# Score products of a query tile issued in turn, and low weight halves of an FFN kept in DRAM, in a two-layer decoder trunk

## The chip, the cores and the metric

The kernel runs on one core of a Trainium2 chip. Its engines are TensorE (PE in the profile, its weight loads PEld), VectorE (DVE), ScalarE (ACT), GpSimd (POOL) and SyncE (SP), which here only issues transfers (DMAs). The metric is the device time of one execution in microseconds; the program is one launch.

## The reference, cut to what matters

Two layers run over 1024 tokens of width 1024. Each layer is a normalised and modulated mixer with a gated residual, then a SwiGLU feed-forward network (FFN) of hidden width 2816, again with a gated residual. The first layer's mixer is half a state-space model, half differential attention with 4 heads; the second layer's is an RWKV-7 recurrence.

```python
# differential attention, one block of 128 queries; c is one of two components of 64 columns
s = jnp.einsum('bqhcd,bkhcd->bhcqk', q_blk, kf[:, :kv_len]) * scale
p = jax.nn.softmax(jnp.where(mask, s, -jnp.inf), axis=-1)
w = p[:, :, 0] - lam * p[:, :, 1]
...
def swiglu(h, w_gate, w_up, w_down):
    return (jax.nn.silu(h @ w_gate) * (h @ w_up)) @ w_down
...
for l in range(DEPTH):
    ...
    x = x + gate_m * mix
    h = rms_norm(x, norm_ffn[l]) * (1.0 + scale_f) + shift_f
    x = x + gate_f * swiglu(h, ffn_w_gate[l], ffn_w_up[l], ffn_w_down[l])
```

## The kernel before

The 1024 tokens are two blocks of 512. Dense products take their operands as two rounded halves: `wsplit` (L442) loads a tile of weights with SP (`wraw`, L446), ScalarE casts it to the high half (`whi`, L449), and VectorE, or GpSimd where the caller says so, subtracts to get the low half (`wlo`, L450). Each of the three tags has two buffers, so a tile's buffer is free again when the tile two before it is done with. `mm3g` (L460) then issues three products per 128 rows of weights: high by high, high weight by low activation, low weight by high activation (L466). A gate or up tile is 1024 rows by 128 columns (512 KB, 24 products), a down tile 384 or 512 rows by 128 columns (9 or 12 products).

The FFN (`ffn`, L495) walks 22 columns of tiles in six chunks; a chunk is the gate and up tiles of 3 or 4 columns, then eight down tiles. Both blocks of tokens use the same weights, each in a pass of its own, so each weight tile is loaded and split twice.

The order of the work is written as generators that are woven: `weave(main, fill, rate)` takes `rate` steps of `fill` for each step of `main`, and a step of an FFN is three products. From the end of the first mixer on, TensorE's instructions stand in the order of the code (`manual_schedule`); the other engines' order, and TensorE's before that point, is set by a scheduler that models the run. The stages that matter here, with their times in the profiled execution:

- 210 to 400 us: attention of the first four query tiles (512 tokens) of each head, between the projections that feed it. TensorE's order is the scheduler's.
- 400 to 520 us: the gated unit of block 0, the output projection, and the first steps of the attention of block 1. TensorE's order is still the scheduler's.
- 520 to 1010 us: block 0's pass of the first layer's FFN (its weight halves split by VectorE), woven with the attention of block 1's query tiles (until 780 us) and then with the second layer's modulation vectors (`mods_acc`, 48 tiles of 512 KB that GpSimd's queue loads, 750 to 920 us).
- 1226 to 1907 us: block 0's recurrence (`rwkv_algebra`, 16 units of short dependent steps over TensorE, VectorE, ScalarE and GpSimd) with block 1's pass of the first layer's FFN as filling, whose low halves GpSimd makes.
- 2124 to 2780 us: the same for block 1's recurrence, filled with block 0's pass of the second layer's FFN, less its last eight down tiles.

In the attention, `attn_scores` (L988) takes one query tile of one head: for each of the two components it takes a bank pair `sps`, issues the products of the queries and keys (64 rows of the array: component 0 on rows 0 to 63, component 1 on rows 64 to 127; L1001) in pieces of at most 512 keys, adds the causal mask of the last 128 keys with a product by the identity (L1006), and then VectorE takes the maximum (L1010) and ScalarE the exponential (L1015). After each component it yields, so that other work stands between the two components. Values (L1039, L1044) follow one step later, the output transpose (L1062) two steps later.

SP issues in its own order and waits in it: a load that waits for its buffer holds back all that stand behind it on SP, which are the weight tiles and, in the recurrence, the loads `ks`, `rr`, `RV`, `wa`, `g2w` of its units and the store `zd`.

Of the kernel before, what the change touches and what calls it, by code (L numbers as in the profile page):

```python
# [8 lines left out]
F32 = mybir.dt.float32  # L9
# [9 lines left out]
P = 128  # L19
D = 1024  # L20
S = 1024
KT = D // P
TB = 512
# [66 lines left out]
def chain(*gens):  # L90
    for g in gens:
        yield from g


def lockstep(*gens):

    gens = list(gens)
    while gens:
        for g in gens[:]:
            if next(g, gens) is gens:  # L100
                gens.remove(g)
        yield
# [19 lines left out]
class Tall:  # L122


    def __init__(self, tiles):
        self.t = tiles
# [20 lines left out]
class Trunk:  # L147
    def __init__(self, ctx, tc, A, out, stages):
        self.ctx, self.tc, self.nc, self.A, self.out = ctx, tc, tc.nc, A, out
        self.stages = stages  # L150
        self.nid = 0
        self.guards = []

    def nm(self, s):
        self.nid += 1
        return f"{s}_{self.nid}"
# [282 lines left out]
            yield  # L439


    def wsplit(self, src, shape, eng=None):  # L442

        nc = self.nc
        raw = self.wp.tile(shape, F32, tag="wraw", name=self.nm("wraw"))
        nc.sync.dma_start(raw, src)  # L446
        hi = self.wp.tile(shape, F32R, tag="whi", name=self.nm("whi"))
        lo = self.wp.tile(shape, F32R, tag="wlo", name=self.nm("wlo"))
        nc.scalar.copy(hi, raw)  # L449
        (eng or nc.vector).tensor_tensor(lo, raw, hi.bitcast(F32), op=ALU.subtract)  # L450
        return hi, lo

    def mm3(self, out, whi, wlo, xhi, xlo, nk, first=True, last=True):

        drain(self.mm3g(out, whi, wlo, xhi, xlo, nk, first, last))
# [37 lines left out]
    def ffn(self, l, st, chunks, eng=None, parts="ud", dtag="B"):  # L493

        nc, A = self.nc, self.A  # L495
        wg, wu, wd = A["ffn_w_gate"][l], A["ffn_w_up"][l], A["ffn_w_down"][l]
        gate = self.mod[l][:, 40:48]
        tp, x = self.tp, st["x"]
        hh, hl = st["h"]
        if "d" not in st:  # L500
            st["d"] = [self.page([P, 4, TB], F32R, "dd", dtag) for _ in range(2)]
        dd = st["d"]
        for f0, f1 in chunks:
            nf = f1 - f0
            for f in range(f0, f1) if "u" in parts else ():
                yield from next(self.inject, ())
                pp, gens = [], []
                for w, nme in ((wg, "pg"), (wu, "pu")):
                    hi, lo = self.wsplit(w[:, f * P : (f + 1) * P].rearrange("(k p) n -> p k n", p=P), [P, KT, P], eng)
                    pt = self.ps.tile([P, TB], F32, tag="mm", name=self.nm(nme))  # L510
                    g = self.mm3w(pt, hi, lo, hh, hl, KT)
                    if f:
                        yield from g
                    gens.append(g)
                    pp.append(pt)
                if not f:
                    yield from lockstep(*gens)

                sg = tp.tile([P, TB], F32, tag="t0", name=self.nm("sg"))
                nc.scalar.activation(sg, pp[0], AF.Tanh, scale=0.5)  # L520
                nc.vector.scalar_tensor_tensor(sg, sg, 1.0, pp[0], op0=ALU.add, op1=ALU.mult)  # L521
                hd = tp.tile([P, TB], F32, tag="t1", name=self.nm("hd"))
                nc.vector.scalar_tensor_tensor(hd, pp[1], 0.5, sg, op0=ALU.mult, op1=ALU.mult)
                nc.scalar.copy(dd[0][:, f - f0, :], hd)
                nc.vector.tensor_tensor(dd[1][:, f - f0, :], hd, dd[0][:, f - f0, :].bitcast(F32), op=ALU.subtract)
            if "d" in parts:

                def down(n):
                    hi, lo = self.wsplit(
                        wd[f0 * P : f1 * P, n * P : (n + 1) * P].rearrange("(k p) n -> p k n", p=P), [P, nf, P], eng  # L530
                    )
                    pd = self.ps.tile([P, TB], F32, tag="mm", name=self.nm("pd"))
                    yield from self.mm3w(pd, hi, lo, dd[0], dd[1], nf)
                    nc.vector.scalar_tensor_tensor(x[:, n, :], pd, gate[:, n : n + 1], x[:, n, :], op0=ALU.mult, op1=ALU.add)  # L534
                    if l == 0 and f1 == NF:
                        self.square(x[:, n, :], n)

                d0, d1 = down(0), down(1)
                yield from self.some(d0, nf - 1)
                yield from self.some(d1, nf - 1)  # L540
                yield from chain(d0, d1, *(down(n) for n in range(2, KT)))
# [446 lines left out]
    def attn_scores(self, b, hd, i, st, ap, pss):  # L988
        nc = self.nc
        v = nc.vector  # L990
        qT, kT = self.qT[b], self.kT[hd // 2]
        kv = (i + 1) * P
        o = i * P - b * TB
        st["pe"], st["l"] = [], []
        for c in range(2):
            r = 64 * c
            sp = pss.tile([P, S if b else TB], F32, tag="s", name=self.nm("sps"))
            for c0 in range(0, kv, 512):
                n = min(512, kv - c0)
                last = c0 + n >= kv  # L1000
                nc.tensor.matmul(  # L1001
                    sp[:, c0 : c0 + n], lhsT=qT[r : r + 64, hd, o : o + P], rhs=kT[r : r + 64, hd % 2, c0 : c0 + n],
                    start=True, stop=not last, skip_group_check=True,
                )
                if last:
                    nc.tensor.matmul(  # L1006
                        sp[:, i * P : kv], lhsT=self.ident_b, rhs=self.cmask, start=False, stop=True, skip_group_check=True
                    )
            mx = ap.tile([P, 1], F32, tag="mx", name=self.nm("mx"), bufs=4)
            v.tensor_reduce(mx, sp[:, 0:kv], axis=AX.X, op=ALU.max)  # L1010
            nm = ap.tile([P, 1], F32, tag="nmx", name=self.nm("nmx"), bufs=4)
            v.tensor_scalar(nm, mx, -0.125, None, op0=ALU.mult)
            pe = self.pe[c][:, self.ne % 2, :]
            l = ap.tile([P, 1], F32, tag="l", name=self.nm("l"), bufs=6)
            nc.scalar.activation(pe[:, 0:kv], sp[:, 0:kv], AF.Exp, bias=nm, scale=0.125, accum_out=l)  # L1015
            st["pe"].append(pe)
            st["l"].append(l)
            yield
        self.ne += 1
# [843 lines left out]
```

## Time and profile before

| what | value |
|---|---|
| median of 3 runs | 3262.19 us (3261.68 to 3269.7) |
| profiled execution | 3254.43 us, span 3252.6 us |
| TensorE busy | 3020.0 us (93%), weight loads 2255.1 us |
| VectorE busy | 1988.2 us (61%) |
| ScalarE busy | 1135.6 us (35%) |
| GpSimd busy | 913.8 us (28%) |
| moved by DMA | 338.47 MB, mean 104 GB/s |
| mean granted TensorE clock | 0.964 |

The clock that the profile grants TensorE has two levels, 1.2 and 2.4 GHz; 0.964 is the mean over the span with 1 for 2.4 GHz. A matmul's time in the timeline runs from its start to its modelled end, and the next one starts before that end; a row that merges several runs from the first start to the last end. A product in full float32 is two matmul instructions. Names such as `pd<-dd,whi` say what is written and read.

### The profile page before, as it was taken

To read this page: it belongs to the slowest core of one execution; us is meant where nothing else is said; L and a number is where in the kernel's file an instruction comes from. 1 tells how busy PE (TensorE), PEld (TensorE's weight loads), DVE (VectorE), ACT (ScalarE), POOL (GpSimd) and SP (SyncE) were. 2 spreads that over 40 slices of the span, in tenths; PEclk is the share of its full clock that TensorE was granted. 3 is DMA by queue.
4 is the path that set the end of the run, shared out by engine and by line. 5 is a ranking of instruction groups with operands and counts; after the bars stand their busy time and mean duration, and the time that the engine had idled before them with its cause. 6 is when DMAs were issued, how large, how long until landed. Compare 5 with 4: busy or idle time off the path is not lost. (4 is left out here: it accounts for less than half of the span.)

```text
span 3252.6 us, 52003 instructions
## 1 busy us (share of the span) xinstructions
PE 3020.0 (93%) x19966; PEld 2255.1 (69%) x19966; DVE 1988.2 (61%) x4013; ACT 1135.6 (35%) x2286; POOL 913.8 (28%) x1034
## 2 busy tenths in 40 slices
PE   5789999998999999999899999999999999999999
PEld 2678866776777676666666776666666667777777
DVE  7754655556665556777777456467777774444443
ACT  3212443333224543333333246433333332322222
POOL 6643310001103103443433441034434334300000
PEclk7889998999999999999999999999999999999999
DMA  7753221226555441221221254422212212533333
GB/s 250 220 118 68 72 79 46 80 72 194 183 167 162 142 137 58 66 74 58 79 66 55 80 171 130 149 61 68 74 53 83 69 53 80 170 89 93 97 101 94
DMA packets 489864, 338.47 MB, mean 104 GB/s; under 512 B 44280, under 2 KB 451088, under 8 KB 488592
## 3 DMA queue, kind: packets, MB, share of 16 engines
q1 hardware_dynamic: 474288, 304.75, 31.2%
q0 software_dynamic: 7632, 25.64, 2.5%
q10 hardware_dynamic: 7696, 4.74, 0.6%
q8 instruction: 159, 2.61, 0.3%
q14 instruction: 89, 0.73, 0.1%
HBM read 292.59 MB, written 42.47 MB: 103 GB/s over the span
## 5 line engine op out<-in xcount | busy, mean ns | idle before, releaser
L449 ACT CAST whi<-wraw 128x1024 fp32r<-128x1024 f32 (+2 forms) x472 | 401.8, 852 | 896.3 <-PE pd L466 186.4
L466 PE MATMUL pd<-dd,whi 128*128 128x512 f32 x1408 | 464.0, 411 | 16.3 <-DVE x L534 12.2
L450 POOL TENSOR_TENSOR wlo<-wraw,whi 128x1024 fp32r<-128x1024 f32 (+2 forms) x184 | 326.6, 1776 | 483.1 <-ACT whi L449 403.1
L450 DVE TENSOR_TENSOR wlo<-wraw,whi 128x1024 fp32r<-128x1024 f32 (+2 forms) x288 | 297.4, 1033 | 264.0 <-ACT whi L449 252.3
L466 PE MATMUL pg<-fhi,whi 128*128 128x512 f32 x704 | 304.9, 433 | 13.2 <-DVE sg L521 10.8
L466 PEld LDWEIGHTS pd<-dd,whi 128*128 128x128 f32 x1408 | 253.4, 189 | 83.3 <-ACT whi L449 16.3
L466 PE MATMUL pu<-fhi,whi 128*128 128x512 f32 x704 | 298.8, 424 | 1.3 <-ACT ev L1359 0.6
L466 PE MATMUL pg<-fhi,wlo 128*128 128x512 f32 x704 | 284.9, 405 | 6.3 <-DVE wlo L450 6.3
L466 PE MATMUL pu<-fhi,wlo 128*128 128x512 f32 x704 | 281.6, 400 | 4.0 <-POOL wlo L450 2.4
L466 PE MATMUL pg<-flo,whi 128*128 128x512 f32 x704 | 283.4, 403 | 0.0
L466 PE MATMUL pd<-dd,wlo 128*128 128x512 f32 x704 | 279.2, 397 | 2.6 <-DVE wlo L450 2.1
L466 PE MATMUL pu<-flo,whi 128*128 128x512 f32 x704 | 280.8, 399 | 0.0
L534 DVE SCALAR_TENSOR_TENSOR x<-pd,mod,x 128x512 f32<-128x512 f32 x192 | 143.4, 747 | 125.3 <-PE pd L466 124.3
L466 PE MATMUL pkrv<-xh,whi 128*128 128x512 f32 x384 | 163.7, 426 | 12.5 <-ACT ev L1359 6.8
L466 PEld LDWEIGHTS pg<-fhi,whi 128*128 128x128 f32 x704 | 136.4, 194 | 49.0 <-DVE sg L521 11.9
L466 PEld LDWEIGHTS pg<-fhi,wlo 128*128 128x128 f32 x704 | 136.2, 193 | 40.6 <-DVE wlo L450 8.7
L466 PEld LDWEIGHTS pd<-dd,wlo 128*128 128x128 f32 x704 | 133.2, 189 | 39.2 <-DVE wlo L450 6.4
L466 PEld LDWEIGHTS pu<-fhi,whi 128*128 128x128 f32 x704 | 133.9, 190 | 37.8 <-issue 3.0
L466 PEld LDWEIGHTS pu<-fhi,wlo 128*128 128x128 f32 x704 | 134.5, 191 | 36.6 <-POOL wlo L450 3.3
L466 PE MATMUL pkrv<-xh,wlo 128*128 128x512 f32 x384 | 153.2, 399 | 2.5 <-DVE wlo L450 2.5
L466 PEld LDWEIGHTS pg<-flo,whi 128*128 128x128 f32 x704 | 137.0, 195 | 25.4
L466 PEld LDWEIGHTS pu<-flo,whi 128*128 128x128 f32 x704 | 134.9, 192 | 25.7
(459 smaller groups left out, 6116.0 us busy)
## 6 DMA issues: line engine op xcount, KB each, us to landing
wraw<-in_ffn_w_gate SPq DMA_DIRECT2D x88, 512.0 KB, 3.8
wraw<-in_ffn_w_up SPq DMA_DIRECT2D x88, 512.0 KB, 3.8
wraw<-in_ffn_w_down SPq DMA_DIRECT2D x128, 256.0 KB, 2.6
mwt<-in_w_ada POOLq DMA_DIRECT2D x48, 512.0 KB, 5.3
mwt<-in_w_ada SPq DMA_DIRECT2D x32, 512.0 KB, 5.8
wraw<-in_ffn_w_down SPq DMA_DIRECT2D x64, 192.0 KB, 2.3
kd<-ev SPq DMA_DIRECT2D x48, 256.0 KB, 2.0
xs<-x SPq DMA_DIRECT2D x8, 1024.0 KB, 5.6
```

The lines of the kernel that those rows point to most:

```text
L449: nc.scalar.copy(hi, raw)
L450: (eng or nc.vector).tensor_tensor(lo, raw, hi.bitcast(F32), op=ALU.subtract)
L466: nc.tensor.matmul(out, lhsT=w(k), rhs=x(k), start=first and i == 0, stop=last and i == n - 1)
L534: nc.vector.scalar_tensor_tensor(x[:, n, :], pd, gate[:, n : n + 1], x[:, n, :], op0=ALU.mult, op1=ALU.add)
```

## The change

Two things are changed. In `attn_scores` both bank pairs are taken first; then, piece by piece of 512 keys, component 0's product and component 1's follow each other; then come the two masks; the maximum and the exponential of each component follow as before, with the yields where they were.

In block 0's pass of the first layer's FFN each of the 92 low halves (44 of 128x1024, 16 of 128x384 and 32 of 128x512) is stored to a DRAM tile `wld` after it is made; SP issues the store when the next `wsplit` is called, behind that call's load. In block 1's pass the subtraction is left out and SP loads the low half from `wld` instead; the load of the raw tile and the cast stay. The second layer's FFN is as it was.

```diff
-    def wsplit(self, src, shape, eng=None):
+    def wsplit(self, src, shape, eng=None, key=None):
...
         nc.scalar.copy(hi, raw)
+        if key in self.los:
+            nc.sync.dma_start(lo.bitcast(F32), self.los.pop(key))
+            return hi, lo
+        self.flush_lo()
         (eng or nc.vector).tensor_tensor(lo, raw, hi.bitcast(F32), op=ALU.subtract)
+        if key is not None:
+            self.unsaved = key, lo, shape
         return hi, lo
+
+    def flush_lo(self):
+        if self.unsaved is not None:
+            key, lo, shape = self.unsaved
+            self.los[key] = self.dr.tile(shape, F32, name=self.nm("wld"))
+            self.nc.sync.dma_start(self.los[key], lo.bitcast(F32))
+            self.unsaved = None
...
-                    hi, lo = self.wsplit(w[:, f * P : (f + 1) * P].rearrange("(k p) n -> p k n", p=P), [P, KT, P], eng)
+                    hi, lo = self.wsplit(
+                        w[:, f * P : (f + 1) * P].rearrange("(k p) n -> p k n", p=P), [P, KT, P], eng, None if l else (nme, f)
+                    )
...
-                        wd[f0 * P : f1 * P, n * P : (n + 1) * P].rearrange("(k p) n -> p k n", p=P), [P, nf, P], eng
+                        wd[f0 * P : f1 * P, n * P : (n + 1) * P].rearrange("(k p) n -> p k n", p=P), [P, nf, P], eng,
+                        None if l else (f0, n),
...
-        for c in range(2):
-            r = 64 * c
-            sp = pss.tile([P, S if b else TB], F32, tag="s", name=self.nm("sps"))
-            for c0 in range(0, kv, 512):
-                n = min(512, kv - c0)
-                last = c0 + n >= kv
+
+        sps = [pss.tile([P, S if b else TB], F32, tag="s", name=self.nm("sps")) for _ in range(2)]
+        for c0 in range(0, kv, 512):
+            n = min(512, kv - c0)
+            for c, sp in enumerate(sps):
+                r = 64 * c
                 nc.tensor.matmul(
                     sp[:, c0 : c0 + n], lhsT=qT[r : r + 64, hd, o : o + P], rhs=kT[r : r + 64, hd % 2, c0 : c0 + n],
-                    start=True, stop=not last, skip_group_check=True,
+                    start=True, stop=c0 + n < kv, skip_group_check=True,
                 )
-                if last:
-                    nc.tensor.matmul(
-                        sp[:, i * P : kv], lhsT=self.ident_b, rhs=self.cmask, start=False, stop=True, skip_group_check=True
-                    )
+        for sp in sps:
+            nc.tensor.matmul(
+                sp[:, i * P : kv], lhsT=self.ident_b, rhs=self.cmask, start=False, stop=True, skip_group_check=True
+            )
+        for c, sp in enumerate(sps):
             mx = ap.tile([P, 1], F32, tag="mx", name=self.nm("mx"), bufs=4)
```

On TensorE, a query tile of the second head in block 0's FFN pass (768 keys) begins before the change with component 0 (`sps_5545`; `wt` are the transposes of the weights of the query tile ahead, `pg` is the FFN):

```order
L1062 MATMUL ot_5526<-ident,os_5494 128x128
L1039 MATMUL wt_5538<-ident,pe_2842 128x128 x4
L1001 MATMUL sps_5545<-kT_1507,qT_1506 128x512
L1001 MATMUL sps_5545<-kT_1507,qT_1506 128x256
L1006 LDWEIGHTS ident_b
L1006 MATMUL sps_5545<-cmask,ident_b 128x128
L466 MATMUL pg_5516<-fhi_5266,whi_5512 128x512
```

Twelve FFN products and the four value products `po` later stands component 1 (`sps_5571`):

```order
L1044 MATMUL po_5537<-vt_1508,wts_5543 128x128 x4
L1001 MATMUL sps_5571<-kT_1507,qT_1506 128x512
L1001 MATMUL sps_5571<-kT_1507,qT_1506 128x256
L1006 LDWEIGHTS ident_b
L1006 MATMUL sps_5571<-cmask,ident_b 128x128
L466 MATMUL pg_5516<-fhi_5267,whi_5512 128x512
```

After the change the same query tile stands in one place (`sps_5549` is component 0, `sps_5550` component 1; the lines are those of the changed file):

```order
L1058 MATMUL wt_5542<-ident,pe_2842 128x128 x4
L1019 MATMUL sps_5549<-kT_1507,qT_1506 128x512
L1019 MATMUL sps_5550<-kT_1507,qT_1506 128x512
L1019 MATMUL sps_5549<-kT_1507,qT_1506 128x256
L1019 MATMUL sps_5550<-kT_1507,qT_1506 128x256
L1024 LDWEIGHTS ident_b
L1024 MATMUL sps_5549<-cmask,ident_b 128x128
L1024 LDWEIGHTS ident_b
L1024 MATMUL sps_5550<-cmask,ident_b 128x128
L481 MATMUL pg_5520<-fhi_5270,whi_5514 128x512
```

Component 1's products moved up past 12 FFN products and the values, next to component 0's of the same size, and the two masks stand behind all four. It is so for all 12 query tiles of block 1 in the heads 1 to 3. Of head 0's four, which the scheduler places, one is fully in pairs and one has one pair of its two; of block 0's 16 query tiles, eight are.

On SP, the start of block 0's FFN pass stands before as follows:

```order
L446 DMA wraw_5428<-in_ffn_w_gate 128x8x128
L446 DMA wraw_5435<-in_ffn_w_up 128x8x128
L446 DMA wraw_5510<-in_ffn_w_gate 128x8x128
L446 DMA wraw_5584<-in_ffn_w_up 128x8x128
L446 DMA wraw_5627<-in_ffn_w_gate 128x8x128
L446 DMA wraw_5696<-in_ffn_w_up 128x8x128
L446 DMA wraw_5753<-in_ffn_w_down 128x3x128
```

After the change (`wld` are the DRAM tiles):

```order
L448 DMA wraw_5428<-in_ffn_w_gate 128x8x128
L448 DMA wraw_5435<-in_ffn_w_up 128x8x128
L465 DMA wld_5440<-wlo_5431 128x1024
L448 DMA wraw_5512<-in_ffn_w_gate 128x8x128
L465 DMA wld_5517<-wlo_5438 128x1024
L448 DMA wraw_5588<-in_ffn_w_up 128x8x128
L465 DMA wld_5593<-wlo_5515 128x1024
L448 DMA wraw_5633<-in_ffn_w_gate 128x8x128
L465 DMA wld_5638<-wlo_5591 128x1024
L448 DMA wraw_5708<-in_ffn_w_up 128x8x128
L465 DMA wld_5713<-wlo_5636 128x1024
L448 DMA wraw_5763<-in_ffn_w_down 128x3x128
```

A store stands between every two weight loads, and the load behind it waits for the same subtraction as it does.

On SP, in block 1's FFN pass beside the recurrence, a stretch before:

```order
L1423 DMA wa_3078_14263<-in_od_a 64x128
L1420 DMA RV_13804<-kd 128x256
L446 DMA wraw_13909<-in_ffn_w_gate 128x8x128
L1692 DMA g2w_13777<-in_od_g 128x128
L1714 DMA zd<-yq_13340 128x256
L1420 DMA ks_14257<-kd 128x256
L1420 DMA rr_14258<-kd 128x256
L446 DMA wraw_14036<-in_ffn_w_up 128x8x128
L446 DMA wraw_14194<-in_ffn_w_down 128x4x128
```

The same stretch after the change:

```order
L1442 DMA wa_3170_14447<-in_od_a 64x128
L453 DMA wlo_13826<-wld_6888 128x1024
L448 DMA wraw_14093<-in_ffn_w_gate 128x8x128
L1439 DMA RV_13988<-kd 128x256
L1711 DMA g2w_13961<-in_od_g 128x128
L1733 DMA zd<-yq_13524 128x256
L1439 DMA ks_14441<-kd 128x256
L453 DMA wlo_13948<-wld_6933 128x1024
L1439 DMA rr_14442<-kd 128x256
L448 DMA wraw_14220<-in_ffn_w_up 128x8x128
L453 DMA wlo_14096<-wld_7008 128x1024
L448 DMA wraw_14378<-in_ffn_w_down 128x4x128
```

The loads `wlo<-wld` stand between; the weight loads and the recurrence's `rr` now stand behind one that waits for TensorE to be done with the low half of two tiles before.

## Rows read from the trace of the kernel before

**Rows 1.** Windows: us, busy us by engine, clock, DMA share, GB/s

```profile
400.00:520.00 120.00, 108.61 (x486) 74.92 (x486) 70.47 (x161) 51.25 (x117) 21.08 (x19) 0.91 0.25 75
...
520.00:740.00 220.00, 216.83 (x970) 162.15 (x969) 120.68 (x227) 81.24 (x158) 7.96 (x14) 0.98 0.22 65
740.00:930.00 190.00, 172.82 (x960) 133.19 (x959) 131.05 (x165) 53.31 (x81) 27.11 (x50) 0.96 0.66 205
...
1226.00:1907.00 681.00, 637.46 (x5388) 454.12 (x5387) 469.95 (x1106) 233.41 (x572) 280.54 (x266) 0.96 0.24 71
...
2124.00:2780.00 656.00, 613.59 (x5292) 435.13 (x5291) 458.69 (x1093) 222.63 (x553) 262.81 (x250) 0.97 0.23 67
```

**Rows 2.** TensorE's timeline: start us, us, line, out<-in, xcount

```profile
325.01 0.48 PE L1001 MATMUL sps<-kT,qT 64*128 64x128 f32 x2
...
348.58 1.12 PE L1001 MATMUL sps<-kT,qT 64*128 64x512 f32 x2
...
587.87 1.98 PE L1001 MATMUL sps<-kT,qT 64*128 64x512 f32 x4
...
602.71 1.34 PE L1001 MATMUL sps<-kT,qT 64*128 64x512 f32 x4
```

**Rows 3.** TensorE's timeline, recurrence: its first pair, then the whole group

```profile
1404.18 0.38 PE L1493 MATMUL pA<-AR,FS 64*128 64x128 f32 x2
...
1404.18 1.16 PE L1493 MATMUL pA<-AR,FS 64*128 64x128 f32 x16
```

**Rows 4.** VectorE groups, 1226 to 1907 us: busy us, mean ns

```profile
L1575 DVE TENSOR_TENSOR XE<-X,cstt 128x256 f32<-128x256 f32 x64 | 35.9, 561 | 1.5
...
L525 DVE TENSOR_TENSOR dd<-hd,dd 128x512 fp32r<-128x512 f32 x22 | 32.3, 1470 | 6.1 <-ACT dd L524 6.1
...
L1464 DVE TENSOR_TENSOR FS<-lwt,L 64x256 f32<-64x256 f32 x30 | 22.4, 746 | 0.3
...
L1468 DVE SCALAR_TENSOR_TENSOR AR<-kk,Wx 64x256 f32<-64x256 f32 x30 | 16.7, 557 | 0.2
```

**Rows 5.** Single lines, ns min/median/max; L525 after 2850 us

```profile
L525 DVE TENSOR_TENSOR dd<-hd,dd x22: 683/686/693, 2872.7 to 3219.6; 128x512 fp32r<-128x512 f32 x22
...
L1464 DVE TENSOR_TENSOR FS<-lwt,L x30: 406/422/2506, 1256.2 to 1779.9; 64x256 f32<-64x256 f32 x30
...
L1575 DVE TENSOR_TENSOR XE<-X,cstt x64: 412/425/2610, 1226.6 to 1807.7; 128x256 f32<-128x256 f32 x64
```

**Rows 6.** Timeline at 1243 us: GpSimd, VectorE, TensorE

```profile
1242.62 4.85 POOL L450 TENSOR_TENSOR wlo<-wraw,whi 128x1024 fp32r<-128x1024 f32 x2 [1.18 <-PE pA L1590]
...
1242.91 2.33 DVE L1575 TENSOR_TENSOR XE<-X,cstt 128x256 f32<-128x256 f32 x1
...
1245.90 0.79 PE L466 MATMUL pg<-fhi,whi 128*128 128x512 f32 x1 [3.31 <-DVE sg L521]
```

**Rows 7.** Chain of waits, 2124 to 2780 us, shares by line

```profile
by line: PE pu L466 16.3%; PE pg L466 15.7%; PE pd L466 11.9%; DVE FS L1464 4.7%; issue 2.9%; PE pA L1493 2.4%; DVE AR L1468 2.4%; PE pR L1649 2.4%; PE pR L1665 2.2%; PE pA L1590 2.1%; PE pY L1667 2.1%; DVE XE L1575 2.0%; DVE kr L1457 1.7%;
```

**Rows 8.** DMA issues in 740 to 960 us: xcount, KB, median us to landing

```profile
wraw<-in_ffn_w_gate SPq DMA_DIRECT2D x11, 512.0 KB, 5.5
wraw<-in_ffn_w_up SPq DMA_DIRECT2D x11, 512.0 KB, 5.4
wraw<-in_ffn_w_down SPq DMA_DIRECT2D x19, 256.0 KB, 2.6
```

**Rows 9.** Windows of 20 us in that stretch

```profile
760.00:780.00 20.00, 14.80 (x69) 11.86 (x68) 12.84 (x15) 6.16 (x8) 4.75 (x8) 0.91 1.08 307
...
840.00:860.00 20.00, 15.00 (x60) 10.40 (x58) 11.51 (x14) 2.92 (x5) 2.65 (x5) 1.00 0.87 277
```

**Rows 10.** Groups of a down tile, and its load's landing

```profile
L450 POOL TENSOR_TENSOR wlo<-wraw,whi 128x512 fp32r<-128x512 f32 x32 | 41.3, 1291 | 71.9 <-ACT whi L449 64.4 <-PE pR L1659 7.5
...
L449 ACT CAST whi<-wraw 128x512 fp32r<-128x512 f32 x136 | 84.3, 620 | 264.0 <-PE pd L466 118.7 <-PE pg L466 45.4 <-PE pu L466 37.1
...
wraw<-in_ffn_w_down SPq DMA_DIRECT2D x20, 256.0 KB, 2.6
```

More of the change, by code (lines that the diff above doesn't have):

```diff
@@ L152, in __init__ @@
         self.guards = []
+        self.los, self.unsaved = {}, None
     def nm(self, s):
```

## The prediction

> **What bounds the kernel now.** I read the windows by stage first, since the change touches three stages with different limits. From 520 to 740 us, the attention of block 1's query tiles in block 0's FFN pass, TensorE is busy for 216.8 of 220 us [rows 1]: time taken from TensorE there comes off the end. From 740 to 930 us it is busy for 172.8 of 190, with the DMA share at 0.66: here transfers are a second limit. From 1226 to 1907 us, the recurrence with block 1's FFN pass, TensorE is busy for 637.5 of 681 us at a mean granted clock of 0.96, VectorE for 470, GpSimd for 280.5, and DMA at 0.24 [rows 1]: TensorE is the bound, but it stands still now and then for the short steps of the recurrence. The chain of waits shows which: it reaches back through the twin stage (2124 to 2780 us, same work, same helpers), and beside the FFN's products VectorE's lines FS, AR and XE stand on it with 4.7, 2.4 and 2.0% [rows 7]. So I look at three things: TensorE's time for the scores, VectorE's time beside GpSimd's subtractions, and the room on the DMA engines.
>
> **The score products.** A product of 64 rows is two instructions in float32. For one component and 512 new keys the pair takes 1.12 us, for 128 keys 0.48 us, and the two pieces of 1024 and 640 keys take 1.98 and 1.34 us [rows 2]. That is TensorE's own time: the four instructions follow each other. The profile shows what the same array does when its halves alternate: in the recurrence, pA's products also have 64 rows and 128 columns of weights and alternate between the two halves, and two of them start within the first 0.1 us; all 16 take 1.16 us [rows 3]. The first 0.48 us pays for two instructions of 128 columns, so 16 one after the other would take 0.48 plus 14 steps; the step, from the rows of 128 and 512 columns, is (1.12 - 0.48)/(2 x 384) = 0.83 ns a column, 0.107 us for 128 columns, so 1.97 us against 1.16. The halves run side by side. After the change a query tile's second component then costs TensorE nothing but one more mask behind the others, a product of one instruction of 128 columns. Its price lies between 0 and 0.27 us, what the first row holds beside its two steps (0.48 - 2 x 0.107); I take 0.16.
>
> In the heads 1 to 3 of block 1 all 12 query tiles are in pairs, in TensorE's fixed order. One component's rows run from 1.34 us (640 keys) to 1.98 us (1024) in equal steps, 6.6 us for the four tiles of a head: 3 x 6.6 = 19.9 us go and 12 x 0.16 = 1.9 come, net 18. Head 0 has one tile in pairs (1.34 us) and half of another (0.86): 2. Block 0's eight paired tiles (two of 128 keys, three of 256, two of 384, one of 512, at 0.48 to 1.12 us) are worth 6.2 us, but where TensorE is busy for 108.6 of 120 us [rows 1] and waits for chains, I count a third, 2. Sum for this part: **-22 us**. The bounds: 0 if the halves do not run side by side at 512 columns (the recurrence shows it at 128), -28 if all is won. Component 1's products now need their banks one round sooner; the exponential that frees them ended some four rounds of FFN work before, so I cost this at nothing.
>
> **Block 1's pass without subtractions.** GpSimd loses its 91 subtractions there. TensorE hardly waits for them, but VectorE does. At 1242.62 us GpSimd starts two of them; VectorE's XE, which takes 0.425 us at the median, takes 2.33, and the FFN's gate behind it on VectorE is late, so that TensorE stands for 3.31 us and takes 0.79 us for its next product at the lower of its two clock levels [rows 5, 6]. The means show how often: dd 1470 ns against 686 where GpSimd rests, XE 561 against 425, FS<-lwt 746 against 422, AR<-kk 557 against the same 422 (same size) [rows 4, 5]. On VectorE's clock that is 22 x 0.784 + 64 x 0.136 + 30 x 0.324 + 30 x 0.135 = 17.2 + 8.7 + 9.7 + 4.1 = 40 us. Only what lies on the chain counts. There FS has 4.7% of 656 us = 30.8, AR 15.7, XE 13.1 [rows 7]; with the excess of each, 324/746 for the one FS and half as much over both kinds (0.30), 0.24 and 0.24, that is 9.2 + 3.8 + 3.1 = 16 us. dd, whose excess is the largest, is cut off from that row; I add 3 for it. **-19 us**. Bounds: -40 (all of VectorE's excess, with TensorE's clock following) and 0 (TensorE's own order takes its place).
>
> The Trainium skill, "SBUF — State Buffer", "Who interferes with whom", says that a VectorE instruction with two SBUF inputs and a GpSimd instruction that reads SBUF exclude each other for a whole instruction, while DMA has ports of its own. The trace agrees with the first half (2.33 against 0.425 us); no row here shows the second, and by it the loads that replace the subtractions would slow no engine.
>
> What takes the subtraction's place is a load that cannot start before TensorE is done with the low half two tiles back. For most tiles that leaves one tile's time, and a down tile lands in 2.6 us [rows 10]; hidden. Where a chunk's third down tile begins, the first two end one right after the other, and there is no cover: before, cast and subtraction took 0.62 + 1.29 = 1.91 us, now 2.6 [rows 10], 0.7 us in each of six chunks: **+4 us**. Bounds 0 and +48, the latter under the rivals. ScalarE's cast and the raw load stay.
>
> **Block 0's pass with stores.** The stores move as much as the weight loads. Up to 740 us the DMA share is 0.22 [rows 1], and doubling it is hidden: a low half's buffer is needed again only two tiles later. From 740 to 960 us the loads are 11 x 512 + 11 x 512 + 19 x 256 KB, 16.5 MB [rows 8], and so the stores. DMA there has bursts with the modulation tiles: 1.08 share at 307 GB/s in 760 to 780 us and 0.87 in 840 to 860, and in both TensorE is busy for only 15 of 20 us [rows 9]. In those 40 us the stores bring 16.5 x 40/220 = 3 MB, 9.8 us at 307 GB/s, of which I charge nearly all: **+9 us**. Bounds: 0 (they fit between the bursts) and +54 (16.5 MB, all in line). The skill's "DMA: Bandwidth & Descriptors", "Specifications", gives 435 GB/s for the fabric; by it the bursts would have room, and the sum would be 9 us lower. The full share at 307 GB/s says otherwise, and I go by that.
>
> **The sum.** -22 - 19 + 4 + 9 = -28 us on the profiled execution's 3254.4 (span 3252.6 and 1.8 around it): 3226. The median of the runs shown is 7.8 us higher, so 3234 us is what I expect of timed runs; the ranges below have that offset in them.
>
> **The rivals.** *VectorE's relief is given back.* GpSimd's other work in the recurrence stays, and TensorE is already busy for 94% of that stage; then the -19 falls away: 3253 us. For it speaks that DVE lines with the excess are under a tenth of the chain; against it the stall of 3.31 us seen whole.
> *VectorE's relief counts in full.* All 40 us come off, since each late step also costs clock (0.79 against about 0.4 us a product): 3234 - 21 = 3213.
> *SP's order turns on the recurrence (slower).* SP waits in order, and each load `wlo<-wld` waits for TensorE to free a buffer. Behind it stand `rr` and the next raw tile; if a unit's operands come late, TensorE, whose order is fixed, waits for the unit. At 3 us for each of 16 units that is +48: 3282 us. It turns slower than before once the delay passes 28 us, some 1.8 us a unit. Against it: raw loads waited on SP for GpSimd's subtractions before, and the loads are small beside a DMA share of 0.24.
> *The halves do not overlap at 512 columns.* Then the first part gives nothing: 3256, no change.
>
> **How the numbers follow.** What a measurement can tell from no change is about 0.3%, so 3252.4 and 3272. Forecast 0.45 (own range 3215 to 3251), relief given back 0.2 at 3253, relief in full 0.2, SP's order 0.1, no overlap 0.05. Faster: nearly all of the forecast, all of the full relief and half of the one at 3253, 0.75. Slower: 0.1. Within: 0.15. The range that leaves out 2 in 10 goes from 3200 to 3262.
>
> **What would show it.** In the profile after: a query tile's scores of 1024 keys should take about 2.0 us for both components in one row of eight instructions, not two rows of 1.98. From 1226 us the recurrence should be some 15 us shorter than its twin, which keeps its subtractions and stood 25 us below it before; dd should be near 0.69 us there, XE near 0.43. The stretch from 740 to 960 us should be longer by about 9 us, with the DMA share near 0.9. It is wrong if VectorE's means fall and the stage does not, if TensorE waits there for `wlo<-wld` or for `ks` and `rr`, or if the scores' rows do not halve.

## The result and the profile after

The kernel after takes 3233.2 us at the median (3223.9 to 3238.8, four runs) against 3265.9 us (3261.7 to 3273.8) before: a ratio of 0.9896, with a 95% interval from 0.9878 to 0.9914. The forecast was 3234 us. The total came out right; of its terms one was about right, one was too small on the side of the gain, and one too small on the side of the cost. The two profiled executions lie closer together than the medians: their spans are 3252.6 and 3234.7 us, 17.9 apart, because 9.7 us were lost in a stretch ahead of the FFN that takes one of two forms (the last experiments).

The windows of the kernel after, by the same stages as in [rows 1] with their new borders (us, busy us of PE, PEld, DVE, ACT and POOL, mean granted clock, DMA share, GB/s):

```profile
400.00:530.00 130.00, 117.65 (x492) 79.58 (x490) 70.76 (x164) 52.22 (x120) 21.01 (x19) 0.80 0.26 77
530.00:738.00 208.00, 198.86 (x980) 153.34 (x977) 120.45 (x231) 81.97 (x161) 7.75 (x14) 1.00 0.44 136
738.00:1016.00 278.00, 251.17 (x1408) 194.31 (x1405) 164.87 (x211) 75.89 (x113) 35.16 (x55) 0.96 0.76 242
...
1234.00:1882.00 648.00, 619.09 (x5386) 439.96 (x5385) 420.06 (x1106) 234.21 (x572) 119.96 (x175) 1.00 0.43 127
2101.00:2760.00 659.00, 612.06 (x5293) 434.75 (x5292) 463.73 (x1094) 222.70 (x553) 261.47 (x250) 0.97 0.23 67
```

The recurrence took 681 us before and takes 648. TensorE's busy time in it fell by 18.4 us (637.46 to 619.09) though it has the same work: its granted clock rose from 0.96 to 1.00 (in a second profile of the same kernel 0.99, with 624.4 us busy). Its idle time fell from 43.5 to 28.9 us. The twin, which keeps its subtractions, stands where it was (656 and 659).

The scores of a 1024-key tile, in TensorE's timeline (start us, us, xcount):

```profile
586.57 1.99 PE L1019 MATMUL sps<-kT,qT 64*128 64x512 f32 x8
588.49 0.28 PE L1024 MATMUL sps<-cmask,ident_b 128*128 128x128 bf16 x2
```

Both components together take the 1.98 us that one took alone [rows 2]: the halves of the array run side by side at 512 columns, as the forecast read from [rows 3] at 128.

VectorE's groups in the recurrence after (busy us, mean ns), to be set against [rows 4]:

```profile
L1594 DVE TENSOR_TENSOR XE<-X,cstt 128x256 f32<-128x256 f32 x64 | 27.1, 423 | 1.5
...
L542 DVE TENSOR_TENSOR dd<-hd,dd 128x512 fp32r<-128x512 f32 x22 | 16.2, 736 | 5.1 <-ACT dd L541 5.1
...
L1483 DVE TENSOR_TENSOR FS<-lwt,L 64x256 f32<-64x256 f32 x30 | 12.5, 417 | 0.4
L1487 DVE SCALAR_TENSOR_TENSOR AR<-kk,Wx 64x256 f32<-64x256 f32 x30 | 12.5, 415 | 0.2
```

And the place of [rows 6] after, in the timeline: XE takes 0.42 us, and TensorE goes on at the higher of its two levels.

```profile
1244.16 0.42 DVE L1594 TENSOR_TENSOR XE<-X,cstt 128x256 f32<-128x256 f32 x1
1244.18 0.48 PE L481 MATMUL pg<-fhi,whi 128*128 128x512 f32 x1
```

What TensorE waited for in the recurrence (total us, times, longest), first before:

```profile
PE pR L1665 <- DVE XU L1661: 23.0, 21, 3.7
PE pR L1649 <- DVE XH L1672: 9.6, 6, 2.7
```

then after:

```profile
PE pR L1684 <- DVE XU L1680: 11.7, 15, 1.6
PE pd L481 <- DMA wlo<-wld: 4.7, 4, 1.7
PE pR L1668 <- DVE XH L1691: 2.4, 5, 0.6
...
PE pu L481 <- DMA wlo<-wld: 1.5, 1, 1.5
```

These two waits for VectorE fell from 32.6 to 14.1 us (all that end with VectorE: from 40.7 to 20.5), and the loads that take the subtraction's place brought 6.6 us of new ones, 0.4 of them in a `pg`.

### The profile page after: what moved, and what is told of

Read it like the earlier page. It is cut to its first block, busy times and chain, and to the rows that moved or that the text cites. A ratio compares the mean times of both kernels' runs of the same rounds, so it can differ in the third digit from the quotient of the medians.

```text
span 3234.7 us, 52231 instructions
## 1 busy us (share of the span) xinstructions
PE 2992.0 (92%) x19966; PEld 2238.2 (69%) x19966; DVE 1945.1 (60%) x4013; ACT 1136.1 (35%) x2286; POOL 750.8 (23%) x942
## 5 line engine op out<-in xcount | busy, mean ns | idle before, releaser
L481 PE MATMUL pd<-dd,whi 128*128 128x512 f32 x1408 | 464.7, 411 | 23.0 <-DVE x L552 14.6
L481 PE MATMUL pg<-flo,whi 128*128 128x512 f32 x704 | 280.4, 398 | 0.0
L456 POOL TENSOR_TENSOR wlo<-wraw,whi 128x1024 fp32r<-128x1024 f32 (+2 forms) x92 | 162.9, 1772 | 247.7 <-ACT whi L451 207.5
L1535 POOL TENSOR_TENSOR hrp<-hrs,mhalf 128x4 f32<-128x4 f32 x64 | 65.7, 1026 | 378.4 <-DVE hrs L1531 220.0
L481 PE MATMUL pkrv<-xl,whi 128*128 128x512 f32 x384 | 153.0, 398 | 0.0
```

The source lines that it names most:

```text
L481: nc.tensor.matmul(out, lhsT=w(k), rhs=x(k), start=first and i == 0, stop=last and i == n - 1)
L1535: nc.gpsimd.tensor_tensor(rp, rs, self.mhalf[:, 0:1].to_broadcast([P, 2 * nt]), op=ALU.pow)
```

## The experiments

All stage times in one table, from the first instruction of a stage to the first of the next on TensorE, in the profiled execution of each kernel. "To FFN": `pout` to the first FFN's first `pg`. "Scores": from there to the last score product. "Stores": from there to the next `pout`. "Recurrence" and "twin": first `pg` to `pout`.

| kernel | to FFN | scores | stores | recurrence | twin | span |
|---|---|---|---|---|---|---|
| before | 107.5 | 227.2 | 260.6 | 680.7 | 655.7 | 3252.6 |
| after | 117.2 | 208.5 | 277.5 | 648.1 | 658.4 | 3234.7 |
| after, again | 106.6 | 207.2 | 278.9 | 651.5 | 658.9 | 3230.8 |
| scores alone | 117.2 | 205.8 | 264.0 | 679.8 | 651.0 | 3244.2 |
| halves alone | 107.4 | 228.9 | 270.5 | 652.3 | 651.9 | 3241.1 |
| stores unused | 117.3 | 207.1 | 281.9 | 677.8 | 655.6 | 3267.9 |
| GpSimd kept | 108.9 | 210.8 | 284.0 | 681.9 | 646.8 | 3256.2 |
| old order outside | 103.8 | 211.9 | 280.4 | 649.9 | 653.0 | 3229.5 |
| fourth chunk not stored | 106.7 | 207.9 | 274.6 | 661.6 | 652.6 | 3238.1 |
| stores later | 117.1 | 206.7 | 271.2 | 651.5 | 658.2 | 3232.3 |
| VectorE subtracts | 118.2 | 208.4 | 262.7 | 665.1 | 660.4 | 3237.1 |
| last two but one combined | 120.1 | 208.5 | 270.5 | 648.8 | 657.2 | 3240.4 |
| and twin on VectorE | 104.1 | 207.0 | 268.3 | 649.9 | 648.2 | 3207.0 |

("Last two but one combined" is old order outside and stores later.) A column's scatter is what kernels show that don't differ in that stage: 647 to 660 us in the twin, 648 to 652 in the recurrence.

The border between "scores" and "stores" moves with the order of the products. Before, twelve FFN products and eight instructions of `po` stand ahead of the last component 1; with the new order they stand behind it. In the trace before they take 3.9 us:

```profile
743.43 0.71 PE L466 MATMUL pd<-dd,whi 128*128 128x512 f32 x2
...
747.31 1.98 PE L1001 MATMUL sps<-kT,qT 64*128 64x512 f32 x4
```

So where a kernel with the new order is set against one with the old, about 4 us of the fall in "scores" are no gain and come back in "stores". The scores alone show it: 264.0 us in "stores", 3.4 above before, without a single store.

**The scores alone.** The kernel before, with the new order of the products.

```diff
...
+        for c0 in range(0, kv, 512):
...
+            for c, sp in enumerate(sps):
...
```

> The kernel before with the new order of the score products alone; no stores, GpSimd subtracts in block 1's pass. The prediction's sum gives -22: 3244 us. What the trace after suggests is -19 in the heads 1 to 3 of block 1 (520 to 740 us), and a question about the stretch before it: there (from 430 us) TensorE stayed at the lower clock level for 44 us instead of 14, which cost some 10 us. If that belongs to the new order of the products: about 3257 us and again over 30 us at the lower level from 430 us. If it was an accident of that one execution: about 3247 us and some 14 us there. The stage of the recurrence (pg's start to pout's start) stays near 681 us by either.

3237.8 us against 3249.4 beside it; ratio 0.9974 (0.9961 to 0.9988). The scores' stage is 21 us shorter, less the 4 of the border 17 to 18 (18 forecast), the recurrence unchanged. The total gained only some 9 us by the ratio and 12 at the median; in the profiled execution 9.7 us came back in the stretch before the FFN (below), and what that stretch took in the others was not recorded.

**The halves alone.** The kernel after, with the old order of the products.

> The kernel after with the old order of the score products: the low halves are stored and loaded, the scores are as before. By the prediction -19 + 4 + 9 = -6: 3260 us. By the trace after, the recurrence's stage gives -33 and the stores cost +17: 3250 us, recurrence near 648 us at a granted clock near 1.0, block 0's pass with the modulation tiles 17 us longer. The lower clock level from 430 us lasts about 14 us if the new order of the products made it longer, and any length if it was an accident.

3234.9 us against 3249.4 beside it, ratio 0.9960 (0.9944 to 0.9976). The recurrence has nearly the whole gain (652.3), so it doesn't come from the scores. The stage of the stores is 10 us longer than before (270.5).

**The stores alone.** The low halves are written, but block 1's pass subtracts again.

```diff
         if key in self.los:
-            nc.sync.dma_start(lo.bitcast(F32), self.los.pop(key))
-            return hi, lo
+            key = None
```

> The kernel after with its stores made, but block 1's pass subtracts on GpSimd again and loads nothing back: against the run with the scores alone it shows what the stores cost by themselves. By the prediction +9, by the traces of before and after +17 (three quarters of it between 740 and 1016 us). Recurrence near 681 us. If the stores cost nothing by themselves, and the 17 us come from something else (where TensorE's clock falls, or how the modulation tiles meet the FFN's), this run is within 3 us of the run with the scores alone.

3259.3 us, ratio 1.0030 (1.0013 to 1.0047): 21.5 us over the scores alone on the same chip. By the windows of the stage, first the scores alone:

```profile
738.00:1002.00 264.00, 247.69 (x1404) 195.21 (x1403) 165.22 (x211) 76.61 (x113) 33.22 (x56) 0.96 0.59 180
```

then with the stores:

```profile
738.00:1020.00 282.00, 251.58 (x1405) 195.16 (x1404) 165.42 (x211) 76.30 (x113) 35.19 (x55) 0.96 0.74 238
```

18 us longer, of which 4 are TensorE's busy time and 14 its idle time; DMA's share rises from 0.59 to 0.74. Beside the new scores the stores cost twice the 9 us that were charged.

**GpSimd's work kept, its result unread.** The kernel after; GpSimd subtracts as before, in place on the raw tile, and TensorE uses the loaded halves. This separates "VectorE is held" from "the low half comes late".

```diff
             nc.sync.dma_start(lo.bitcast(F32), self.los.pop(key))
+            nc.gpsimd.tensor_tensor(raw, raw, hi.bitcast(F32), op=ALU.subtract)
             return hi, lo
```

> The kernel after, where GpSimd still does block 1's subtractions of the first FFN, but in place on the raw tile, where nothing reads them: TensorE gets the loaded low halves as in the kernel after, and waits for no subtraction. If the gain of the recurrence comes from VectorE no longer being held by GpSimd, it goes: XE near 0.56 us, dd near 1.4 us, windows at the lower clock level come back, recurrence near 675 to 681 us, in all about 3265 us. If it comes from the low halves being there earlier, it stays: recurrence near 648 us, 3234 us.

3260.3 us, ratio 1.0031 (1.0013 to 1.0050): the gain of the recurrence is gone to the last microsecond (681.9). VectorE's groups there are those of [rows 4] again, though nothing reads what GpSimd makes:

```profile
L1595 DVE TENSOR_TENSOR XE<-X,cstt 128x256 f32<-128x256 f32 x64 | 35.9, 561 | 1.5
L543 DVE TENSOR_TENSOR dd<-hd,dd 128x512 fp32r<-128x512 f32 x21 | 31.4, 1495 | 5.2 <-ACT dd L542 5.2
```

TensorE's waits that end with VectorE are back too (38.9 us). Two other ways by which GpSimd's work could delay the recurrence do not show: no wait of VectorE in this stage ends with GpSimd, and TensorE waits neither for a result of GpSimd nor for the cast of a raw tile that GpSimd held. So the gain is VectorE's release. The low half's being early has no part in it that shows.

**The subtractions on VectorE.** The scores alone, with block 1's pass given no engine, so that VectorE subtracts; no stores.

```diff
-later(lambda: self.ffn(0, fs, CHUNKS, pool))
+later(lambda: self.ffn(0, fs, CHUNKS))
```

> The new score order, no stores, and block 1's pass subtracts its low halves on VectorE instead of GpSimd (91 x about 1.03 us = 94 us more on VectorE, which is busy for 420 of 648 us without them). If GpSimd holding VectorE was the whole harm, the recurrence comes out nearer to 648 than to 680 us, and without the 20 us of stores the run is faster than the kernel after. If VectorE's queue then makes the recurrence's steps late (a step behind 1 us of subtraction instead of behind 2.4 us held), it stays near 680 us or above: within 5 us of the run with the scores alone.

3238.5 us against 3262.9, ratio 0.9925 (0.9899 to 0.9951). The recurrence is 665.1: half of the gain, between the two cases that were expected. Without the stores the run is still not faster than the kernel after (0.9896 and 0.9920). VectorE is no longer held, but its own queue is longer:

```profile
L450 DVE TENSOR_TENSOR wlo<-wraw,whi 128x1024 fp32r<-128x1024 f32 (+2 forms) x92 | 85.9, 933 | 18.9 <-ACT whi L449 18.1
...
L1576 DVE TENSOR_TENSOR XE<-X,cstt 128x256 f32<-128x256 f32 x62 | 26.8, 432 | 1.5
L525 DVE TENSOR_TENSOR dd<-hd,dd 128x512 fp32r<-128x512 f32 x22 | 15.3, 696 | 0.7 <-ACT dd L524 0.6
```

and TensorE's waits for `XU` stay near those of before:

```profile
PE pR L1666 <- DVE XU L1662: 18.9, 21, 2.7
```

**The fourth chunk not stored.** If the cost of the stores lies where they meet the modulation tiles, leaving out the 4 gate, 4 up and 8 down tiles of that place should win.

```diff
-None if l else (nme, f)
+None if l or f0 == 10 else (nme, f)
...
-None if l else (f0, n),
+None if l or f0 == 10 else (f0, n),
```

> The kernel after without stores for the fourth chunk (FFN tiles 10 to 13 and their down tiles), whose loads meet the modulation tiles from 760 to 860 us; block 1's pass subtracts these 16 tiles on GpSimd. If the stores cost because they meet the modulation tiles there, the stretch from the last score product to pout falls from 278 to about 266 us, the recurrence grows by a sixth of 33 us (5), and the run is some 5 to 8 us faster than the kernel after (ratio near 0.988). If the cost of the stores is spread evenly over bytes, 18 us for 91 tiles, the skipped 12 give 3 us and 5 come back: 2 to 3 us slower than the kernel after.

3241.4 us, ratio 0.9938 (0.9917 to 0.9960). The theory of the place fell: the stage gained 3 to 4 us where 12 were expected, and the recurrence lost 10 to 13 where a sixth of the gain is 5. Why 16 subtractions bring back more than their share is open. The wait at the first `pu` of this chunk, 5.9 us in the kernel after, is still 5.2 us here (next experiment).

**The stores later.** Each store is issued on SyncE one tile later, behind the raw load that waits for the same subtraction instead of ahead of it.

```diff
...
+        self.unsaved.append((key, lo, shape))
...
+        if len(self.unsaved) > 1:
+            key, lo, shape = self.unsaved.pop(0)
...
```

> The kernel after with each store issued on SyncE one tile later: behind the raw load of the next tile but one, which waits for the same subtraction, and no longer ahead of it. If the stores cost because they go ahead of the raw load that TensorE needs next, the stretch from the last score product to pout falls from 278 to 265 to 270 us and the run is 8 to 12 us faster than the kernel after. If they cost by the share of the DMA engines alone, whatever the order, it stays within 3 us of the kernel after; if the next subtraction but one then waits for the store, it is slower.

The timeline of SyncE's queue in the kernel after shows the longest wait (start us, us of the issue): the store stands 3.21 us at the queue, and the raw load of `pu` is issued behind it.

```profile
752.40 8.40 SPq L1247 DMA_DIRECT2D gluy<-ys  x3
760.90 3.21 SPq L465 DMA_DIRECT2D wld<-wlo  x1
764.21 0.38 SPq L448 DMA_DIRECT2D wraw<-in_ffn_w_up  x1
```

ScalarE's cast of that tile starts at 774.0, and TensorE, which has stood for 5.87 us, takes its next product at the lower level (0.80 us). But the load is not all that holds the cast: four casts of `gluh` stand ahead of it on ScalarE, and when ScalarE is done with them and with `sg`, it waits only 0.56 us more for the load:

```profile
769.04 3.90 ACT L1248 CAST gluh<-gluy 128x512 fp32r<-128x512 f32 x4
...
774.00 1.04 ACT L451 CAST whi<-wraw 128x1024 fp32r<-128x1024 f32 x1 [0.56 <-DMA wraw<-in_ffn_w_up]
```

```profile
775.09 0.80 PE L481 MATMUL pu<-fhi,whi 128*128 128x512 f32 x1 [5.87 <-ACT whi L451]
```

With the stores later the cast stands ahead of `gluh`, and TensorE waits 0.53 us there:

```profile
771.61 1.05 ACT L453 CAST whi<-wraw 128x1024 fp32r<-128x1024 f32 x1 [8.08 <-DMA wraw<-in_ffn_w_up]
...
773.04 4.13 ACT L1248 CAST gluh<-gluy 128x512 fp32r<-128x512 f32 x4
```

ScalarE's order is the scheduler's, and it changed with the kernels. In all six with the new scores and the stores ahead (the fourth chunk not stored among them) `gluh` goes first, and TensorE waits 5.2 to 8.9 us at this `pu`; in the other seven the cast goes first, and the wait is at most 2 us. In two of the six ScalarE did not wait for the load at all, and its order alone held the cast; here with the fourth chunk not stored:

```profile
769.96 1.04 ACT L451 CAST whi<-wraw 128x1024 fp32r<-128x1024 f32 x1
```

```profile
771.06 0.80 PE L481 MATMUL pu<-fhi,whi 128*128 128x512 f32 x1 [5.21 <-ACT whi L451]
```

The landings between 740 and 1010 us (KB, median us), after:

```profile
wld<-wlo SPq DMA_DIRECT2D x24, 512.0 KB, 3.3
...
wraw<-in_ffn_w_gate SPq DMA_DIRECT2D x12, 512.0 KB, 7.3
wraw<-in_ffn_w_up SPq DMA_DIRECT2D x12, 512.0 KB, 5.8
```

and with the stores later:

```profile
wld<-wlo SPq DMA_DIRECT2D x24, 512.0 KB, 5.1
...
wraw<-in_ffn_w_gate SPq DMA_DIRECT2D x12, 512.0 KB, 5.1
wraw<-in_ffn_w_up SPq DMA_DIRECT2D x12, 512.0 KB, 5.0
```

The raw loads land as early as before [rows 8], and the stage falls to 271.2 us, and to 270.5 and 268.3 in the two later kernels with this order, against 277.5 to 284.0 in the five with all stores ahead and the new scores. So about half of the cost went with the orders of SyncE and ScalarE, which changed together; how much is SyncE's alone is not shown. The halves alone have the stores ahead and ScalarE's cast first: 270.5 us, about 274 with the border where the new scores have it, so that 3 to 6 us are left for SyncE's order by that one profile. What remains goes along with the higher DMA share; its cause was not tested. 3224.2 us, ratio 0.9890 (0.9865 to 0.9915): by times alone it can't be told from the kernel after.

**The old order outside.** In the kernel after, the scores alone and the stores unused, TensorE ran at the lower level for over 40 us from 430 us on (the stretch of 117 us instead of 107). The theory: the new order of the products does it, where the scheduler places them.

> The kernel after, but with the old order of the score products wherever the scheduler places them (block 0's tiles and head 0 of block 1); the new order only in heads 1 to 3 of block 1, in TensorE's written order, and the stored halves as they are. Theory: the new order in the scheduled part is what makes TensorE stay at the lower level for 44 us from 430 us on. Then this run has some 14 us there, its stretch from pout's start to the FFN's first pg is 107 to 109 us instead of 117, and it is 8 to 10 us faster than the kernel after (ratio to before near 0.987). Rival: the 44 us come from something else that the changed kernels share; then 117 us stay, and the time is that of the kernel after or 2 us above (ratio 0.990 to 0.993).

3229.9 us, ratio 0.9899 (0.9871 to 0.9928), and the stretch was short (103.8): as the theory said. But with GpSimd kept and with the fourth chunk not stored it was short too (108.9 and 106.7), with the new order, and the next two runs overturned the theory.

**The kernel after again, and the combination.**

> The kernel after itself, beside the combinations below and on their chip, so that they can be set against it. Ratio to before near 0.990. If the 44 us at the lower clock level from 430 us belong to the new order of the score products in the scheduled part, they stand here again (the stretch from pout to pg near 117 us); if they came by accident, they may be away.

> The kernel after with the old order of the score products outside TensorE's written order (as one run before) and each store issued one tile later (as another). In the traces these gave 8 us (the pg of the first FFN at 522 instead of 530 us) and 6 us (271 instead of 277.5 us from the last score product to pout). If they add: 14 us under the kernel after in the profiled span, near 3220 us, ratio to before near 0.986 and some 0.4% under the kernel after. If one undoes the other, or runs differ by more than that: within 0.2% of the kernel after.

The kernel after again took 3244.3 us against 3264.1, ratio 0.9920 (0.9890 to 0.9949), and its profiled execution has the short stretch; the combination, with the old order, has the long one. The windows from 430 to 475 us, of the kernel after:

```profile
430.00:445.00 15.00, 12.13 (x28) 6.55 (x29) 6.08 (x21) 3.72 (x15) 1.10 (x2) 0.51 0.00 1
445.00:460.00 15.00, 13.86 (x37) 7.53 (x37) 8.18 (x25) 5.39 (x16) 1.98 (x2) 0.50 0.01 2
460.00:475.00 15.00, 14.27 (x37) 8.11 (x36) 5.99 (x17) 4.40 (x11) 1.19 (x1) 0.51 0.00 0
```

of the same kernel again:

```profile
445.00:460.00 15.00, 12.96 (x49) 6.65 (x47) 10.05 (x31) 5.51 (x18) 2.66 (x3) 0.90 0.01 2
460.00:475.00 15.00, 13.99 (x67) 9.31 (x67) 11.27 (x26) 9.55 (x21) 3.18 (x3) 1.00 0.16 46
```

and of the combination:

```profile
445.00:460.00 15.00, 14.48 (x30) 7.14 (x30) 6.83 (x22) 4.03 (x15) 1.47 (x2) 0.50 0.00 1
460.00:475.00 15.00, 13.65 (x37) 8.11 (x37) 6.72 (x21) 5.94 (x16) 1.29 (x2) 0.50 0.01 2
```

The same kernel does both, so the order does not decide it. The long form came in 5 of 8 profiled executions with the new order there, and in 1 of 5 with the old one: whether the order shifts the odds stays open. The combination's time, 3223.6 us, ratio 0.9880 (0.9852 to 0.9908), is 20 us under the kernel after beside it, with intervals that just overlap.

**The twin on VectorE.** The combination, and block 1's recurrence also subtracts on VectorE.

```diff
-self.ffn(1, fs, CHUNKS[:-1], pool), self.ffn(1, fs, CHUNKS[-1:], pool, "u")
+self.ffn(1, fs, CHUNKS[:-1]), self.ffn(1, fs, CHUNKS[-1:], None, "u")
```

> The kernel of the run above, and in the twin stage (the recurrence of block 1, whose FFN weights are new, so that no stored halves exist) the subtractions on VectorE instead of GpSimd. In block 0's recurrence that gave 15 us (665 against 680). If the same holds in the twin: 640 us instead of 655 and a total some 15 us under the run above. If VectorE's queue makes TensorE wait for the low halves there: the twin stays near 655 us, no gain.

3209.2 us (3205.2 to 3224.6), ratio 0.9841 (0.9815 to 0.9868): the fastest of all, beating both kernels; its interval lies wholly below that of the kernel after on the same chip. How much of that is the twin's is less sure: 648.2 us is at the low end of what that stage showed without this edit (646.8 to 660.4), and the interval overlaps that of the combination.

## Why the prediction was right, term by term

**The scores, -18 in the heads 1 to 3:** right. 227.2 and 228.9 us with the old order, 205.8 to 211.9 with the new, about -20, of which 4 are the border's, so -16; the 1.99 us for both components is the step itself. TensorE's busy time fell by more (223.9 to 199.4 us, 4 of it the border), but its idle time in the stage rose from 3.2 to 9.1 us, 3.2 of them in one wait of a `pu` behind VectorE's `nmx`, where it had waited 0.4 us. The forecast put nothing for new waits. **The further -4** in the part that the scheduler places can't be told from the scatter: the time to the first `pout` is 414.6 before and 411.6 to 420.1 in the others, and the stretch from there to the FFN, 104 to 120 us, scatters by more than the term. (The rows of block 0's eight tiles add up to 6.0 us, not 6.2; it changes nothing.)

**Block 1's pass, -19 + 4:** the mechanism was right, the size half of what came. The recurrence fell by 29 to 33 us. The step that failed was "only what lies on the chain counts". It took the shares of VectorE's lines on the chain and their excess, 16 us, and left out what TensorE's clock adds (only the 3 us for dd were added). (FS's share of 0.30 does not follow from the rows: its two kinds take 746 and 595 ns, and against 422 that is 0.37, which adds 2 us.) VectorE's means fell by what was forecast (XE 561 to 423, FS 746 to 417, AR 557 to 415, dd 1470 to 736 rather than 686), and TensorE's idle time by 14.6 us, the new waits for loads included, as -19 + 4 has it; but its busy time fell by 18.4 us besides (12.7 in the second profile), since the stage lost nearly all of its time at the lower level. The rival "relief in full" had that, with [rows 6] as its evidence (0.79 us for the product behind the stall), and its -40 + 4 is nearer to the truth. The forecast's own test was at odds with its term: 15 us off a stage that stood 25 us above its twin leaves it 10 above, and the text said 15 below; it came out 10 below. The +4 for the loads was about right: 6.6 us of waits for `wlo<-wld`, the longest 1.7. Such waits were named as a sign of being wrong; at this size they are within the term.

The rule that the prediction cites (the Trainium skill, "SBUF — State Buffer", "Who interferes with whom") is borne out in both halves now: GpSimd's unread subtractions alone bring XE back to 561 ns, and with 0.43 instead of 0.24 of the DMA engines busy, XE takes 423 ns, as at its median before.

**The stores, +9:** the place and the sign were right, the size half. Beside the new scores they cost 17 to 18 us in the stage and 21.5 in the total; beside the old ones the stage grew by 10 (270.5 against 260.6), which is nearly the forecast. What differs between the two is ScalarE's order at the `pu` above, with a wait of 5.2 to 8.9 us that the sum did not have; that it makes the whole difference isn't shown. The DMA share of the stage came out at 0.76, not near 0.9. The step that fell short was "the stores fit outside the two bursts". The kernel with the scores alone has the same order of work without stores; set against it, TensorE is busy for less from 760 to 780 us, but also from 780 to 800 and from 900 to 920 us, outside the two windows that were charged. First the scores alone:

```profile
760.00:780.00 20.00, 17.55 (x76) 14.41 (x76) 12.60 (x15) 9.53 (x13) 3.17 (x6) 0.83 0.86 259
780.00:800.00 20.00, 17.41 (x66) 13.67 (x67) 13.37 (x21) 4.11 (x6) 3.56 (x7) 0.83 0.51 161
...
900.00:920.00 20.00, 19.40 (x143) 14.90 (x142) 17.58 (x21) 4.56 (x8) 2.64 (x5) 1.00 0.71 230
```

then the kernel after:

```profile
760.00:780.00 20.00, 13.57 (x54) 10.23 (x53) 10.18 (x11) 7.36 (x9) 2.11 (x4) 0.74 0.98 301
780.00:800.00 20.00, 14.10 (x54) 11.09 (x54) 14.51 (x22) 3.99 (x7) 6.98 (x9) 0.83 0.75 245
...
900.00:920.00 20.00, 17.37 (x136) 13.69 (x135) 13.84 (x17) 4.87 (x7) 3.17 (x6) 1.00 1.00 350
```

What the sum left out was order: a store stood on SyncE ahead of the raw load that TensorE needed next, and ScalarE's order changed with it.

**The sum.** With the sizes measured it is -20 - 30 + 17 (-16 and +13 with the border put right) and 2 in the projections behind it, -31 us, against -32.7 by the medians; the forecast had -28. It hit in part by luck: the gain missed in the recurrence (15) and the cost missed at the stores (4 in this pair of profiles, 8 against the scores alone) stand on opposite sides; the -4 of the scheduled part can't be seen, and the 9.7 us of the stretch ahead of the FFN, which only some executions have, are in no term. The slower rival, SyncE's order, is refuted in the recurrence (no waits for `ks` or `rr`), but in the stage of the stores SyncE's order was part of the cost.

## What to carry to other kernels

Where an engine stands still in small pieces and its clock falls behind them, price a removed stall with the time at the lower level that it causes: here that about doubled the gain (14.6 us idle, 18.4 busy). An off-path engine can be dear through another engine that it holds; leaving its work in place with nobody reading the result shows this cleanly. A transfer that nobody waits for can still cost when it is issued ahead of one that somebody needs: issued behind, the raw loads landed in 5.1 and 5.0 us instead of 7.3 and 5.8. Before a shorter stage is put down to one engine's order, look at the others': a scheduler may have moved them with the same edit. And where instructions change places, compare stages by the work done, not by the last instruction of a name.

## What was not expected of the hardware

One kernel, twice on the chip, spent 44 us or 14 us at the lower clock level in the same place, and its stretch there took 117.2 or 106.6 us; 0.3% of a time can be this alone. In the long form TensorE was busy for 13.9 and 14.3 of 15 us at the lower level, and the level did not rise in these 30 us. With the low halves loaded the recurrence kept a granted clock of 0.99 to 1.00, with VectorE's subtractions 0.98, with all of GpSimd's 0.96 to 0.97.

The share of the DMA engines does not tell their rate: in the kernel after they moved 301 GB/s at a share of 0.98 and 350 at 1.00 in two windows, before 307 at 1.08 [rows 9]. So the full share at 307 GB/s, by which the forecast sized the stores, is no fixed price of a byte.
